# Cross attention's value products past the first superblock as split products of 512 tokens

## The chip, the core and the metric

The kernel runs on one core of one Trainium2 chip. The metric is the device time of one execution in microseconds (us). The core has a matrix engine (TensorE, PE in the profile, with its weight loads as PEld), a vector engine (VectorE, DVE), a scalar engine (ScalarE, ACT), GpSimd (POOL) and SyncE (SP), which here issues most of the DMA. TensorE reads on-chip memory (SBUF) and writes PSUM, which the others read.

## What is computed

One layer on 2048 tokens of width 1024: a norm, one wide input projection, three branches beside each other, and a gated merge that is projected once more and added to the input. The branches are an RWKV-7 recurrence (8 heads of 64), windowed attention with sinks (8 heads of 64), and cross attention into a memory of 256 tokens (4 heads of 128). The change is in the last one:

```python
def memory_cross_attn(q, mem, mem_norm_g, w_mem_kv, xq_g, xk_g):
    q = rms_norm(q.reshape(bsz, t, X_HEADS, X_HEAD_DIM), xq_g)
    kv = rms_norm(mem, mem_norm_g) @ w_mem_kv
    km, vm = kv[..., :X_WIDTH], kv[..., X_WIDTH:]
    km = rms_norm(km.reshape(bsz, m, X_HEADS, X_HEAD_DIM), xk_g)
    vm = vm.reshape(bsz, m, X_HEADS, X_HEAD_DIM)
    s = jnp.einsum('bthd,bmhd->bhtm', q, km).astype(jnp.float32) * (X_HEAD_DIM ** -0.5)
    p = jax.nn.softmax(s, axis=-1)
    o = jnp.einsum('bhtm,bmhd->bthd', p.astype(vm.dtype), vm)
    return o.reshape(bsz, t, X_WIDTH)
```

All is float32. The last `einsum`, probabilities times the memory's values, is called the value product below.

## The kernel before

**Tiles and split products.** The tokens are worked in four superblocks of 512 (`sb` 0 to 3). Most matrix products are split products: each operand is held as a rounded half of type f32r (ScalarE copies it with `AF.Copy`, which rounds) and the rest (DVE subtracts the rounded half from the original), and `gemm3` (L453 to L459) makes three products of the halves, high by high, high by rest, rest by high, into one PSUM bank. A few products are plain f32: transposes, the recurrence, and cross attention's value products (L1003).

**Weights.** In the first superblock a weight block is loaded raw, split, used, and stored split to DRAM (L438 to L443); later superblocks load the split block (L435). SP issues these loads and stores, in order, from one queue; there are 8 buffers (`whl`).

**Memory keys and values.** `mem_kv` runs once at the start. Keys are kept split in DRAM (`Kd`, named `mk`), values plain (`Vd`, named `mv`, L642): two tiles of 128 memory tokens by 512 channels.

**Two streams.** Within a superblock, `stream_r` (the recurrence: preparation, a forward substitution on DVE at L803 to L805 called the inverse below, then a chain of small products) and `stream_f` (four cross heads, then windowed attention woven with the merges, then gates) are written interleaved; the numbers that they yield and `PACE` set where one stands against the other. Then `order` plans the whole program: `lay_out` takes the next ready instruction of each engine by its rank, with costs of its own for each operation and the free buffers of each pool, and the resulting order of each engine is fixed. So an added or removed instruction can move others anywhere behind it. All engines work through their order without overtaking.

**A cross head** (`cross_head`, L948 on). Loads of the keys `km` and the values `vm` (two buffers of 128x2x128 each, 128 KB); the query projection; its split (L954, L955); statistics; scores by `gemm3`; maximum, exponential and denominators. Then the part in question: per half of 256 tokens, `scaled_by` scales two probability tiles (DVE, L934; in the first superblock ScalarE, L936), four transposes each of 128x128 (L999) put them into a PSUM bank `as_` (two such banks), ScalarE copies the bank to SBUF (L1001), and two plain f32 products of 256 tokens (L1003) accumulate over the 256 memory tokens into the bank `oo` (one such bank). Behind it, `silu2` (L923 to L929) makes the gate: projection into `mm` (two banks), a tanh on ScalarE (L927), a multiply on DVE (L928); L1006 multiplies it with the value product and `split_y` splits the result (L941, L942). The other intermediate tiles, `g2` in the code and `g` in the profile, share 11 buffers of 2 KB per partition.

## Time and profile before

| what | value |
|---|---|
| median of 3 runs | 2250.22 us (2249.85 to 2250.74) |
| profiled execution, own time | 2250.33 us |
| its span, first to last instruction | 2248.5 us |
| busy: PE, DVE, ACT, POOL | 99%, 68%, 41%, 7% of the span |
| mean granted TensorE clock | 0.997 of full |
| moved by DMA | 430.55 MB, mean 191 GB/s |

A timeline row gives start, duration, engine, line, operation, output<-inputs, shape and count, then in brackets the engine's idle time before it and what ended it. Durations of TensorE overlap, since its products are pipelined: what one costs is the difference to the start of the next. A wait row reads "who <- for whom: us in total, times, longest". A windows row gives the stretch, its length, then busy time and count of PE, PEld, DVE, ACT and POOL, the granted clock, the DMA share and GB/s. A chain row gives start, duration and what.

### The profile page before, as it was taken

How to read it: one execution, taken by the hardware profiler on the slowest of the kernel's cores; microseconds unless marked ns; L12 is line 12 of the kernel's file. 1: busy time of each engine (PE TensorE's matmuls, PEld its weight loads, DVE VectorE, ACT ScalarE, POOL GpSimd, SP SyncE). 2: the span in 40 equal slices, each digit the busy share in tenths (PEclk: the TensorE clock that was granted, in tenths of full speed). 3: DMA queues.
4: the chain of work that ended last, by engine and by line, in shares of the span. 5: the costliest groups of instructions: out<-in, count | busy, mean ns of one | idle time of the engine just before them, and what ended most of it. 6: DMA issues, size and time to landing. Idle time of an engine off the chain costs nothing.

```text
span 2248.5 us, 36875 instructions
## 1 busy us (share of the span) xinstructions
PE 2219.2 (99%) x13706; PEld 1806.1 (80%) x13706; DVE 1533.0 (68%) x3951; ACT 926.2 (41%) x2024; POOL 147.9 (7%) x209
## 2 busy tenths in 40 slices
PE   8999999999999999999999999999999999999999
PEld 7888778778888778878888878787888887787887
DVE  7799789775469777953437957985245895896312
ACT  6664565455253354423214345442223435434210
POOL 1000110000000011000000001000000001100000
PEclk9999999999999999999999999999999999999999
DMA  7777546679844444446774434445676444343655
GB/s 230 265 234 241 195 164 226 231 264 356 323 146 161 134 141 149 147 166 234 241 239 136 164 122 150 148 136 194 229 252 198 157 141 160 117 146 132 206 192 192
DMA packets 146226, 430.55 MB, mean 191 GB/s; under 512 B 16640, under 2 KB 21120, under 8 KB 146048
## 3 DMA queue, kind: packets, MB, share of 16 engines
q1 hardware_dynamic: 129920, 398.83, 52.6%
q10 hardware_dynamic: 16128, 29.37, 4.0%
q8 instruction: 109, 1.79, 0.3%
q14 instruction: 69, 0.57, 0.1%
HBM read 333.24 MB, written 94.90 MB: 190 GB/s over the span
## 4 chain that ended last, share of the span: by engine, by line
PE 74%; DVE 18%; ACT 3%; DMA 2%; issue 2%; POOL 1%; SPq 0%; DVEq 0%; ACTq 0%; POOLq 0%
PE mm L457 18%; PE mm L459 18%; PE mm L458 18%; DVE ibc L803 1%; PE rw L881 1%; DVE ibc L804 1%; ACT g L1102 1%; DVE Yi L805 1%; PE mm L1172 1%; PE mm L1174 1%; PE mm L1173 1%; PE oo L1003 1%; PE rw L866 1%; PE rw L874 1%; DVE g L1114 1%
## 5 line engine op out<-in xcount | busy, mean ns | idle before, releaser
L457 PE MATMUL mm<-hH,whl 128*128 128x512 f32 x1888 | 750.4, 397 | 5.8 <-DVE g L928 3.5
L459 PE MATMUL mm<-hH,whl 128*128 128x512 f32 x1888 | 748.9, 397 | 0.0
L458 PE MATMUL mm<-hL,whl 128*128 128x512 f32 x1888 | 748.7, 397 | 0.0
L457 PEld LDWEIGHTS mm<-hH,whl 128*128 128x128 f32 x1888 | 355.1, 188 | 77.9 <-DVE g L928 3.9
L459 PEld LDWEIGHTS mm<-hH,whl 128*128 128x128 f32 x1888 | 355.3, 188 | 69.4
L458 PEld LDWEIGHTS mm<-hL,whl 128*128 128x128 f32 x1888 | 355.3, 188 | 68.3 <-issue 0.7
L439 ACT ACTIVATE whl<-raw 128x512 fp32r<-128x512 f32 x178 | 111.2, 629 | 146.9 <-PE mm L459 80.1
L440 DVE TENSOR_TENSOR whl<-raw,whl 128x512 fp32r<-128x512 f32 x178 | 124.5, 702 | 50.6 <-ACT whl L439 49.5
L457 PE MATMUL mm<-yh,whl 128*128 128x512 f32 x384 | 151.3, 394 | 0.0
L458 PE MATMUL mm<-yl,whl 128*128 128x512 f32 x384 | 150.8, 393 | 0.0
L459 PE MATMUL mm<-yh,whl 128*128 128x512 f32 x384 | 150.7, 393 | 0.0
L872 ACT ACTIVATE SP<-Z,Pl 64x64 f32<-64x64 f32 x256 | 88.3, 345 | 115.0 <-DVE Z L882 111.4
L803 DVE STREAM_SHUFFLE ibc<-Nc 128x496 f32<-128x496 f32 (+30 forms) x248 | 113.4, 473 | 0.1
L1155 DVE SCALAR_TENSOR_TENSOR g<-g,mm 128x512 f32<-128x512 f32 x32 | 21.8, 681 | 128.6 <-PE mm L459 128.5
L804 DVE TENSOR_TENSOR ibc<-ibc,Yi 128x496 f32<-128x496 f32 (+30 forms) x248 | 104.5, 421 | 3.9
L805 DVE TENSOR_TENSOR Yi<-Yi,ibc 128x496 f32<-128x496 f32 (+30 forms) x248 | 103.2, 416 | 0.9
L882 DVE SCALAR_TENSOR_TENSOR Z<-rw,Pl,SP 64x64 f32<-64x64 f32 x224 | 63.5, 284 | 51.1 <-PE rw L881 47.5
L1140 ACT ACTIVATE gt<-mm 128x512 f32<-128x512 f32 x64 | 38.0, 593 | 144.1 <-PE mm L459 143.8
L457 PEld LDWEIGHTS mm<-yh,whl 128*128 128x128 f32 x384 | 72.1, 188 | 15.0 <-DVE g L1155 0.4
L459 PEld LDWEIGHTS mm<-yh,whl 128*128 128x128 f32 x384 | 72.1, 188 | 14.6
L458 PEld LDWEIGHTS mm<-yl,whl 128*128 128x128 f32 x384 | 72.1, 188 | 14.3
L1102 ACT ACTIVATE g<-g,mxs,st 128x256 f32<-128x256 f32 (+1 forms) x128 | 74.5, 584 | 18.4 <-DVE mxs L1095 18.2
(1902 smaller groups left out, 3783.9 us busy)
## 6 DMA issues: line engine op xcount, KB each, us to landing
whl<-k SPq DMA_DIRECT2D x486, 512.0 KB, 3.3
k<-whl SPq DMA_DIRECT2D x162, 512.0 KB, 4.4
raw<-in_w_in SPq DMA_DIRECT2D x118, 256.0 KB, 3.3
g<-in_x ACTq DMA_DIRECT2D x32, 256.0 KB, 4.4
out<-g ACTq DMA_DIRECT2D x32, 256.0 KB, 4.5
raw<-in_w_proj SPq DMA_DIRECT2D x24, 256.0 KB, 3.1
rt<-in_x ACTq DMA_DIRECT2D x24, 256.0 KB, 5.7
rt<-in_xt ACTq DMA_DIRECT2D x24, 256.0 KB, 5.8
```

Of the source, the lines that this page charges most:

```text
L439: S.activation(w[:, 0], raw, AF.Copy)
L440: V.tensor_tensor(w[:, 1], raw, w[:, 0].bitcast(F32), op=ALU.subtract)
L457: PE.matmul(out, lh, rh, start=i == 0, stop=False)
L458: PE.matmul(out, lh, rl, start=False, stop=False)
L459: PE.matmul(out, ll, rh, start=False, stop=i == n - 1)
L803: V.stream_shuffle(bc[:, :, :w], N_[:, :, s + 1:], [s] * 32)
L804: V.tensor_tensor(bc[:, :, :w], bc[:, :, :w], Y[:, :, s:s + 1].to_broadcast([128, n, w]), op=ALU.mult)
L805: V.tensor_tensor(Y[:, :, s + 1:], Y[:, :, s + 1:], bc[:, :, :w], op=ALU.add)
L872: S.activation(SP[h, i], Z[h, i, e, c], AF.Copy, scale=g[4][h, c:c + 1])
L882: upds = [V.scalar_tensor_tensor(Sst[h, g[0]] if c == NC_ - 1 else Z[h, i, e, c + 1], pS[h, i, e], g[4][h, c:c + 1], SP[h, i], op0=ALU.mul ...
L1102: S.activation(prs[b][:, i, m0:], prs[b][:, i, m0:], AF.Exp, scale=r2[:, b, i:i + 1], bias=mx[:, b, i:i + 1], accum_out=mx[:, b, 2 + i:3 + i])
L1140: S.activation(t, gp, AF.Tanh, scale=0.5)
```

## The change

Past the first superblock a head scales all four probability tiles first, makes for each half of the memory tokens (`kt`) four transposes into one bank of 512 tokens, splits that bank (ScalarE copies the rounded half, DVE subtracts), and makes one split product of 512 tokens per `kt`: six f32r products in place of four plain f32 ones of 256 tokens. The values are therefore also kept split in DRAM (`Vs`, named `mvs`), which `mem_kv` writes in four stores. The value tile grows to 128x2x2x128 (256 KB) and has one buffer in place of two. The first superblock computes as before, from the plain values, in a half of the larger tile.

```diff
+    Vs = dp.tile([128, 2, 2, 512], F32, name="mvs")
...
             nc.sync.dma_start(Vd[:, i], t)
+            p = [g2(F32R), g2(F32R)]
+            S.activation(p[0], o[i], AF.Copy)
+            V.tensor_tensor(p[1], o[i], p[0].bitcast(F32), op=ALU.subtract)
+            for u in range(2):
+                nc.sync.dma_start(Vs[:, u, i], p[u].bitcast(F32))
...
-        vm = rp.tile([128, 2, 128], F32, name="vm", bufs=2)
-        nc.sync.dma_start(vm, Vd[:, :, h * 128:(h + 1) * 128])
+        if sb:
+            vm = rp.tile([128, 2, 2, 128], F32R, name="vm", bufs=1)
+            nc.sync.dma_start(vm.bitcast(F32), Vs[:, :, :, h * 128:(h + 1) * 128])
+        else:
+            vm = rp.tile([128, 2, 2, 128], F32, name="vm", bufs=1)[:, 0]
+            nc.sync.dma_start(vm, Vd[:, :, h * 128:(h + 1) * 128])
...
+        if not sb:
...
+        else:
+            for q in range(4):
+                scaled_by(prs[q // 2][:, q % 2], dn[:, q:q + 1], sb)
+            pts = []
+            for kt in range(2):
+                pt = s_ps()
+                for q in range(4):
+                    PE.transpose(pt[:, q * 128:(q + 1) * 128], prs[q // 2][:, q % 2, kt * 128:(kt + 1) * 128], ident)
+                pts.append((g2(F32R), g2(F32R)))
+                S.activation(pts[kt][0], pt, AF.Copy)
+                V.tensor_tensor(pts[kt][1], pt, pts[kt][0].bitcast(F32), op=ALU.subtract)
+            oo = o_ps()
+            gemm3(oo, [((vm[:, 0, kt], vm[:, 1, kt]), pts[kt]) for kt in range(2)])
```

What the planner makes of it is shown at three places. In the changed kernel L1022 is the transpose, L1025 the subtraction, L1030 the old L1006, L934 the old L928, L940 the old L934, L809 to L811 the old L803 to L805, L727 the old L721; the split value products are those of L457 to L459 with output `oo`.

TensorE at head 0 of the second superblock, from its last transposes on, before:

```order
L999 MATMUL as__6868<-c_ident,g_6793 128x128 x2
L999 MATMUL as__6879<-c_ident,g_6796 128x128 x4
L458 MATMUL mm<-hL,whl 128x512
L459 MATMUL mm<-hH,whl 128x512
L457 MATMUL mm<-hH,whl 128x512
L458 MATMUL mm<-hL,whl 128x512
L1003 MATMUL oo<-g_6875,vm 128x256 x2
L1003 MATMUL oo<-g_6886,vm 128x256 x2
```

and now (`g_6889` is a rounded half, `g_6890` its rest):

```order
L1022 MATMUL as__6884<-c_ident,g_6809 128x128
L1022 MATMUL as__6893<-c_ident,g_6809 128x128
L458 MATMUL mm<-hL,whl 128x512
L459 MATMUL mm<-hH,whl 128x512
L457 MATMUL mm<-hH,whl 128x512
L458 MATMUL mm<-hL,whl 128x512
L459 MATMUL mm<-hH,whl 128x512
L457 MATMUL mm<-hH,whl 128x512
L457 MATMUL oo<-g_6889,vm 128x512
L458 MATMUL mm<-hL,whl 128x512
L459 MATMUL mm<-hH,whl 128x512
L458 MATMUL oo<-g_6890,vm 128x512
```

The value products moved two dense products back, and the second one, the first that needs the rest, two more.

DVE at head 2 of the second superblock, from its last scalings on, before (in the middle of the inverse):

```order
L934 TENSOR_SCALAR g_7364<-g_7364,dn 128x256 x2
L804 TENSOR_TENSOR ibc<-ibc,Yi 128x16x27
L803 STREAM_SHUFFLE ibc<-Nc 128x16x26
L805 TENSOR_TENSOR Yi<-Yi,ibc 128x16x27
L804 TENSOR_TENSOR ibc<-ibc,Yi 128x16x26
L803 STREAM_SHUFFLE ibc<-Nc 128x16x25
```

and now:

```order
L940 TENSOR_SCALAR g_7389<-g_7389,dn 128x256 x2
L811 TENSOR_TENSOR Yi<-Yi,ibc 128x16x27
L809 STREAM_SHUFFLE ibc<-Nc 128x16x26
L809 STREAM_SHUFFLE ibc<-Nc 128x16x25
L810 TENSOR_TENSOR ibc<-ibc,Yi 128x16x26
L1025 TENSOR_TENSOR g_7449<-as__7443,g_7448 128x512
L1025 TENSOR_TENSOR g_7458<-as__7452,g_7457 128x512
```

TensorE at the same head, from its last transposes on, before:

```order
L999 MATMUL as__7426<-c_ident,g_7364 128x128 x4
L459 MATMUL mm<-hH,whl 128x512
L457 MATMUL mm<-hH,whl 128x512
L458 MATMUL mm<-hL,whl 128x512
L459 MATMUL mm<-hH,whl 128x512
L1003 MATMUL oo<-g_7422,vm 128x256 x2
```

and now:

```order
L1022 MATMUL as__7452<-c_ident,g_7389 128x128 x2
L457 MATMUL mm<-hH,whl 128x512
L458 MATMUL mm<-hL,whl 128x512
L459 MATMUL mm<-hH,whl 128x512
L457 MATMUL mm<-hH,whl 128x512
L458 MATMUL mm<-hL,whl 128x512
L457 MATMUL oo<-g_7448,vm 128x512
L459 MATMUL mm<-hH,whl 128x512
L457 MATMUL mm<-hH,whl 128x512
L458 MATMUL mm<-hL,whl 128x512
L459 MATMUL mm<-hH,whl 128x512
L458 MATMUL oo<-g_7449,vm 128x512
```

Two subtractions are new on DVE in the middle of the inverse, four of whose steps stand before them, and the second value product has five plus four dense products between it and the transposes.

DVE in the first superblock, in the preparation of the recurrence's second group of heads, with the gate of a windowed head (L928) in it. The last rows before L928, before:

```order
L728 SCALAR_TENSOR_TENSOR QO<-rt,Pt 64x8x64
L730 SCALAR_TENSOR_TENSOR rt<-rt 128x512
L735 TENSOR_TENSOR rk__2989<-rk__2989,rt 128x512
L440 TENSOR_TENSOR whl<-raw,whl 128x512
L732 TENSOR_TENSOR BK<-rt 64x8x64
L742 TENSOR_TENSOR QE<-rr__3114,Pt 64x8x64
L732 TENSOR_TENSOR BK<-rt 64x8x64
L440 TENSOR_TENSOR whl<-raw,whl 128x512
L928 SCALAR_TENSOR_TENSOR g_3505<-g_3505,mm 128x512
```

and now, from the first row (L727, the old L721) that reads the statistics from PSUM:

```order
L727 TENSOR_SCALAR dk<-rw 64x4
L734 SCALAR_TENSOR_TENSOR QO<-rt,Pt 64x8x64
L727 TENSOR_SCALAR dk<-rw 64x4
L736 SCALAR_TENSOR_TENSOR rt<-rt 128x512
L727 TENSOR_SCALAR dk<-rw 64x4
L748 TENSOR_TENSOR QE<-rr__3127,Pt 64x8x64
L728 RECIPROCAL dk<-dk 128x8
L738 TENSOR_TENSOR BK<-rt 64x8x64
L741 TENSOR_TENSOR rk__3002<-rk__3002,rt 128x512
L440 TENSOR_TENSOR whl<-raw,whl 128x512
L934 SCALAR_TENSOR_TENSOR g_3518<-g_3518,mm 128x512
```

Ahead of this piece stand one more L727 and one more L440. Before, the rows of `dk` stood far ahead of L928, with two more products of the recurrence's output (L916, L917) among them; now they stand right before it. On TensorE the products that make those statistics stood nine dense products ahead of the projection that L928 reads, and stand twelve into its 24 now.

More of the change, by code (lines that the diff above doesn't have):

```diff
@@ L991, in cross_head @@
         yield 5.667
[L992 to L1003 removed]
+        if not sb:
+            oo = o_ps()
+            for t2 in range(2):
+                pt = s_ps().rearrange("p (k i t) -> p k i t", k=2, i=2)
+                for i in range(2):
+                    q = 2 * t2 + i
+                    scaled_by(prs[t2][:, i], dn[:, q:q + 1], sb)
+                    for kt in range(2):
+                        PE.transpose(pt[:, kt, i], prs[t2][:, i, kt * 128:(kt + 1) * 128], ident)
+                pts = g2(shape=(128, 2, 256))
+                S.activation(pts.rearrange("p k t -> p (k t)"), pt.rearrange("p k i t -> p (k i t)"), AF.Copy)
+                for kt in range(2):
+                    PE.matmul(oo[:, t2 * 256:(t2 + 1) * 256], vm[:, kt], pts[:, kt], start=kt == 0, stop=kt == 1)
+        else:
+            for q in range(4):
+                scaled_by(prs[q // 2][:, q % 2], dn[:, q:q + 1], sb)
+            pts = []
+            for kt in range(2):
+                pt = s_ps()
[4 more added lines that the diff above has]
+                V.tensor_tensor(pts[kt][1], pt, pts[kt][0].bitcast(F32), op=ALU.subtract)
+            oo = o_ps()
+            gemm3(oo, [((vm[:, 0, kt], vm[:, 1, kt]), pts[kt]) for kt in range(2)])
         yield 3
```

10 lines of the change are left out of this document (removed).

## The prediction

> **What bounds the kernel now.** I read the page's busy times and slices first, then the chain of work that ended last.
>
> ```profile
> span 2248.5 us, 36875 instructions
> PE 2219.2 (99%) x13706; PEld 1806.1 (80%) x13706; DVE 1533.0 (68%) x3951; ACT 926.2 (41%) x2024; POOL 147.9 (7%) x209
> PE   8999999999999999999999999999999999999999
> DVE  7799789775469777953437957985245895896312
> PE 74%; DVE 18%; ACT 3%; DMA 2%; issue 2%; POOL 1%; SPq 0%; DVEq 0%; ACTq 0%; POOLq 0%
> ```
>
> TensorE has work in every slice. VectorE (DVE) is full in some slices and half idle in others, and holds 18% of the chain. So the time is the sum of what TensorE must stream, plus the places where it waits. All listed waits of TensorE come to about 26 us; the two largest groups are these:
>
> ```profile
> PE mm L457 <- DVE g L928: 3.5, 1, 3.5
> PE rw L770 <- DVE whl L761: 2.5, 4, 1.1
> ```
>
> None of the listed waits after the first superblock stands at cross attention's value products. A cheaper product there is therefore worth its own TensorE time, unless a new wait eats it.
>
> **What goes and what comes on TensorE.** The timeline of TensorE at head 2 of the second superblock, with the old products (L1003) between two stretches of dense products:
>
> ```profile
> 707.33 1.89 PE L1003 MATMUL oo<-g,vm 128*128 128x256 f32 x8
> 708.87 0.58 PE L457 MATMUL mm<-hH,whl 128*128 128x512 f32 x1
> 709.28 0.39 PE L458 MATMUL mm<-hL,whl 128*128 128x512 f32 x1
> ...
> 711.59 0.39 PE L459 MATMUL mm<-hH,whl 128*128 128x512 f32 x1
> ```
>
> Durations overlap, so I take differences of starts. From 709.28 to 711.59 there are ten dense products, 0.23 us each. From 707.33 to 709.28 are 1.95 us, in which one dense product (L457) and the eight L1003 records lie: the eight cost 1.95 - 0.23 = 1.72 us, 0.215 each. Each plain f32 product of 256 tokens appears as two records. In its place come six split products of 512 tokens, the form of those dense ones: 6 x 0.23 = 1.38 us. Saved: 0.34 us a head. The group row gives the number of heads:
>
> ```profile
> L1003 PE MATMUL oo<-g,vm 128*128 128x256 f32 x128 | 30.8, 379 | 0.6 <-ACT g L1001 0.6
> ```
>
> 128 records are 16 heads of 8; the first superblock keeps its 4. **12 x 0.34 = 4.1 us saved.** The transposes stay eight a head and of one size (128x128), so I count them at no difference. What the switch between the two kinds of product costs is inside the 1.95 us.
>
> [...]
>
> **What comes on the other engines.** ScalarE's two copies of 512 columns a head stay two. DVE gets two subtractions of 128x512 from PSUM a head; the kernel makes the same operation for the queries (L955):
>
> ```profile
> 647.98 0.69 DVE L955 TENSOR_TENSOR g<-mm,g 128x512 fp32r<-128x512 f32 x1
> ```
>
> 24 x 0.69 = 16.6 us more on DVE, 1.4 a head. What hides them differs by head. At head 0 DVE has nothing to do there:
>
> ```profile
> 642.47 0.68 DVE L778 TENSOR_TENSOR rt<-rr__6859,rt 128x512 fp32r<-128x512 f32 x1
> 645.75 0.69 DVE L1006 TENSOR_TENSOR gt<-oo,gt 128x512 f32<-128x512 f32 x1 [2.60 <-PE oo L1003]
> L1001 ACT ACTIVATE g<-as__6868 x1: 599/599/599, 642.6 to 642.6; 128x512 f32<-128x512 f32 x1
> 642.82 0.48 PE L458 MATMUL mm<-hL,whl 128*128 128x512 f32 x1
> ```
>
> The rounded half is ready at 642.6 + 0.6 = 643.2 and the rest at 643.9, inside the idle 2.60 us. The new order puts six dense products, the first value product and two more dense ones behind the transposes, which end at about 642.8: the product that needs the rest starts at 642.8 + 9 x 0.23 = 644.9, a us after it is there. No wait. At heads 2 and 3 DVE is full:
>
> ```profile
> 680.00:730.00 50.00, 50.00 (x272) 41.75 (x270) 48.75 (x134) 18.45 (x43) 2.71 (x5) 1.00 0.48 161
> 706.09 0.66 DVE L803 STREAM_SHUFFLE ibc<-Nc 128x416 f32<-128x416 f32 x1
> 706.64 0.58 DVE L805 TENSOR_TENSOR Yi<-Yi,ibc 128x432 f32<-128x432 f32 x1
> 705.96 0.60 PE L999 MATMUL as__7426<-c_ident,g 128*128 128x128 f32 x4
> 706.32 0.47 PE L459 MATMUL mm<-hH,whl 128*128 128x512 f32 x1
> ```
>
> (In the first row the columns behind the span are the busy times of PE, PEld, DVE, ACT and POOL; DVE has 48.75 of 50.) At head 2 the new order of DVE puts four steps of the inverse, 0.55 us from start to start, between the last scaling and the two subtractions: the first rest is there 4 x 0.55 + 0.69 = 2.9 us after the scaling. On TensorE four transposes (706.32 - 705.96 = 0.36 us), nine dense products and the first value product stand between that scaling and the second value product, which needs the rest: 0.36 + 10 x 0.23 = 2.7 us. That is even, and a small wait follows. Nothing shows it before; its bounds are 0 and the whole subtraction pair, 1.4 us. I take 0.1 us at heads 2 and 3, nearest to the row of head 0: **+0.6 us** in all. What queues behind the subtractions is the inverse (L803 to L805), so the recurrence starts 1.4 to 2.8 us later in each superblock; TensorE has other streams' dense products to fill with, as it has 50.00 of 50 us in that row.
>
> **The loads.** One buffer of 256 KB in place of two of 128 KB: a head's load may now be issued only when the value products of the head before are done, so its time must fit between two heads.
>
> ```profile
> 643.99 1.73 PE oo L1003 x8
> 667.55 1.73 PE oo L1003 x8
> 707.49 1.73 PE oo L1003 x8
> 727.73 1.73 PE oo L1003 x8
> vm<-mv SPq DMA_DIRECT2D x16, 128.0 KB, 2.5
> SPq L951 <- PE oo L1003: 43.9, 12, 4.8
> ```
>
> The shortest distance is 20.2 us, the load lands in 2.5 us, and twice the bytes in at most 5. The last row says that SP's queue already stood at 12 of these loads, 3.7 us each, for value products of an earlier head, with the weight loads queued behind, and TensorE lists no wait for it. I count 0; the bound is one such stand of 4.8 us at a place where weights run short.
>
> **The memory's part.** Two copies on ScalarE, two subtractions and four stores of 256 KB at about 50 us.
>
> ```profile
> mv<-g SPq DMA_DIRECT2D x2, 256.0 KB, 5.0
> 0.00:60.00 60.00, 54.22 (x287) 46.73 (x288) 42.39 (x113) 37.33 (x81) 11.15 (x27) 0.91 0.72 240
> ```
>
> The last two numbers are the DMA share and GB/s. 1 MB at 240 GB/s is 4.4 us of transfer, with 28% of the share free; a bound of 4.4 us therefore, and 0 below. TensorE keeps working there on weights loaded before, so I take **+0.3 us**, near the lower end.
>
> **The sum.** The profiled execution took 2250.33 us by its own time, span 2248.5; the median of three runs is 2250.22, the same within 0.1. 2250.3 - 4.1 + 0.6 + 0.3 = **2247.1 us**. A measurement of this kernel tells about 0.2% (4.5 us) from no change, so this saving, if it comes as worked out, lies within it.
>
> **Rivals.** (a) *A stall in the first superblock goes, or only its clock loss.* One TensorE wait there is dear:
>
> ```profile
> 289.23 0.15 DVE L721 TENSOR_SCALAR dk<-rw 64x4 f32<-64x4 f32 x1
> 299.02 0.69 DVE L928 SCALAR_TENSOR_TENSOR g<-g,mm 128x512 f32<-128x512 f32 x1
> 295.87 0.39 PE L459 MATMUL mm<-hH,whl 128*128 128x512 f32 x1
> 299.76 0.53 PE L457 MATMUL mm<-hH,whl 128*128 128x512 f32 x1 [3.50 <-DVE g L928]
> 300.10 0.62 PE L458 MATMUL mm<-hL,whl 128*128 128x512 f32 x1
> 300.51 0.63 PE L459 MATMUL mm<-hH,whl 128*128 128x512 f32 x1
> 300.00:304.00 4.00, 4.00 (x15) 2.77 (x16) 3.42 (x8) 1.50 (x5) 0.00 (x0) 0.57 0.65 211
> ```
>
> 3.5 us idle, and then products at 0.41 instead of 0.23 us at a granted clock of 0.57 over 4 us, another 1.7 us. [...] All 5.2 us are freed if DVE's L928 comes early enough: 2247.1 - 5.2 = **2241.9**; the clock loss alone, 2245.4. The new order changes this place. TensorE makes the statistics on which the first dk row (L721) waits 21 dense products later, 12 before the end of the projection that L928 reads. From that dk row to the twin of L928 stand seven operations of 0.69 us and five small ones of 0.15 (itself among them), 5.6 us, where before it was 299.02 - 289.23 = 9.8. So the twin begins 5.6 - 12 x 0.23 = 2.8 us behind the projection's end; before it began 299.02 - 296.1 = 2.9 behind. The stall stays, most likely. Chance 0.12.
>
> (b) *DVE becomes the bound in the later superblocks.* The chain of the second superblock runs through DVE for over 100 us, here its first and last piece,
>
> ```profile
> 818.39 0.73 DVE g L573 x2
> 926.81 0.61 DVE g L509
> ```
>
> and DVE may reach it 1.4 us late per subtraction pair. If nothing hides any pair, all 16.6 us show: 2247.1 + 16.6 - 0.6 = 2263.1; if half does, **2254.8**, slower than before. It decides from 4.1 / 3 = 1.4 us of new wait per superblock on. For it: DVE 48.75 of 50. Against it: the window of 800 to 900 us leaves DVE a fifth idle,
>
> ```profile
> 800.00:900.00 100.00, 98.40 (x588) 80.01 (x587) 79.80 (x184) 45.22 (x100) 12.40 (x16) 1.00 0.44 148
> ```
>
> and TensorE idles only 1.6 us there. Chance 0.14.
>
> (c) *The saving is given back.* The products are cheaper, but TensorE waits for the rest halves by the same 0.34 us, or the rearranged first superblock loses as much: **2250.3**. Chance 0.16.
>
> (d) *The new products stream faster than the dense ones,* at the 0.215 us that the eight old records show: 12 x (1.72 - 1.29) = 5.2 saved, **2246.0**; chance 0.06. [...]
>
> **How the numbers follow.** The forecast has 0.52, with its own range 2245 to 2249, of which I put 0.12 below 2245.7 (a saving of over 0.2%). Faster by over 0.2%: 0.12 from (a), 0.12 of the forecast, 0.03 of (d): 0.27. Slower by over 0.2%, above 2254.7: 0.09 of (b), 0.02 of (c): 0.11. Within: 0.62. The range runs from 2242.5 (leaving out half of (a)) to 2253 (leaving out most of (b)): it takes in +4.4 of the memory's part and, with the other sums, the bound of 4.8 us.
>
> **What would show it.** Right: a head's six products between dense ones cost 1.38 us from start to start, no wait of over 0.3 us at the second of them, waits of TensorE at about 26 us in all, the 3.5 us wait in the first superblock still there, with the reduced clock behind it. Wrong: six products far from 1.38 us; new waits for DVE that recur in three superblocks at the same place; the clock row lower or higher than before; waits for weights behind the load of the values.

## The result, and the profile after

The changed kernel took 2252.99 us (median of 22 executions, 2249.59 to 2259.96), the kernel before beside it 2250.83 (22 executions, 2249.66 to 2253.55). The ratio is 1.0014, 95% interval 1.0008 to 1.0020: a little slower, though within the 0.2% that I had set as the bound. 2247.1 was forecast. The spread is part of the result: it was 3.9 us before and is 10.4 us now. The profiled execution of the changed kernel took 2254.41 us by its own time, 4.1 more than the profiled one of before, where the medians differ by 2.2: nine of the 22 executions had a mean granted clock of 0.996 or less, with a median of 2256.07, and the profiled one is among them; the other 13 have a median of 2251.84.

The page of the changed kernel, its busy times and the engines' shares of the chain of work that ended last:

```profile
span 2252.3 us, 36907 instructions
PE 2216.2 (98%) x13682; PEld 1803.8 (80%) x13682; DVE 1548.9 (69%) x3977; ACT 922.0 (41%) x2024; POOL 154.7 (7%) x209
PE 75%; DVE 18%; ACT 2%; DMA 2%; issue 1%; POOL 1%; SPq 0%; DVEq 0%; ACTq 0%; POOLq 0%
```

TensorE has less to do (24 matmuls fewer, 3.0 us less busy) and the span is 3.8 us longer. Both can only hold if it waits more. The waits of TensorE in the changed kernel, those that are new or longer:

```profile
PE mm L457 <- DVE g L934: 4.6, 1, 4.6
PE rw L759 <- DVE QO L748: 2.9, 3, 1.0
PE rw L791 <- DVE carry L667: 2.5, 3, 0.8
PE as__3855 L1110 <- DVE g L1084: 1.6, 1, 1.6
PE as__19826 L511 <- DVE g L509: 0.9, 1, 0.9
PE as__9438 L511 <- DVE g L509: 0.9, 1, 0.9
PE as__14632 L511 <- DVE g L509: 0.9, 1, 0.9
```

Three of them come once in each later superblock (L759, L791, L511: 1.0, 0.8 and 0.9 us); two stand in the first superblock (L457 with 4.6 us in place of 3.5, and L1110 with 1.6, which is new). None stands at the value products, and none is for a weight or a value tile. All listed waits of TensorE add up to about 31 us, against about 25 before.

To see how much each stretch gained or lost I cut all traces at the same places. A superblock ends where its output projection starts its last product (L1174 before, L1198 in the changed kernel); its output phase begins at its last transposes of the recurrence's result (L525), and in the last superblock, which has none there, three dense products before the first product of `yh` (2178.40 us before, 2182.36 in the changed kernel). Windows from the end of one superblock to the next output phase, the three later superblocks summed, before:

```profile
sum 1437.36, PE 1429.22 PEld 1160.05 DVE 976.98 ACT 567.19 POOL 99.63; mean PE 476.41 PEld 386.68 DVE 325.66 ACT 189.06 POOL 33.21
```

and in the changed kernel:

```profile
sum 1436.79, PE 1424.94 PEld 1155.22 DVE 991.31 ACT 564.75 POOL 105.48; mean PE 474.98 PEld 385.07 DVE 330.44 ACT 188.25 POOL 35.16
```

The first number is the length, the next the busy time of TensorE, so the difference is its idle time. TensorE saves 4.3 us there, as the forecast's 4.1 said, and idles 11.85 in place of 8.14 us, 3.7 more. So 0.6 us is left of the saving. The other 4.5 us of difference stand in the first superblock: it ends at 608.1 us before and at 612.6 in the changed kernel. TensorE's idle time there is 19.6 in place of 16.6 us, and the clock is halved (granted 0.50) for 17.1 in place of 13.7 us. In such a stretch a dense product starts every 0.43 us (300.16 to 304.43 us in the changed kernel, ten steps) in place of 0.23. Half clock for 3.4 us more therefore costs 1.7 us, an estimate of half its length, and 3.0 + 1.7 = 4.7 us is about what is seen. This is a balance of two things: in the first 25 us of the program the clock is halved for 3.4 us in place of 10.2, and at 300 and 340 us for 13.7 in place of 3.4, so a better start hides part of what these two places cost. The output phases differ by 0.3 us in all.

These are the two places in the changed kernel's timeline where the first superblock's new waits stand, with what is beside them. The first three rows show the wait for the windowed head's gate (L934, the old L928), the last two the new wait at L1110:

```profile
299.57 0.80 PE L457 MATMUL mm<-hH,whl 128*128 128x512 f32 x1 [4.62 <-DVE g L934]
300.16 0.63 PE L458 MATMUL mm<-hL,whl 128*128 128x512 f32 x1
300.58 0.63 PE L459 MATMUL mm<-hH,whl 128*128 128x512 f32 x1
...
337.40 0.95 PE L499 MATMUL as__3843<-c_bones,g 128*128 128x2 f32 x8
339.99 0.45 PE L1110 MATMUL as__3855<-KsH,g 128*128 128x128 f32 x1 [1.64 <-DVE g L1084]
```

and the two windows of halved clock:

```profile
298.70:305.53 6.83, 5.96 (x16) 4.39 (x18) 5.96 (x14) 1.12 (x2) 0.00 (x0) 0.50 0.32 115
339.65:346.48 6.83, 6.50 (x43) 6.08 (x44) 5.07 (x14) 0.24 (x1) 1.91 (x2) 0.50 0.90 299
```

The seventh value, 0.50, is the granted clock. Before, there was one such window of 3.41 us at 300 us and none at 340.

### The profile page after: what moved, and what is told of

It is laid out like the page before. It is cut to its first block, busy times and chain, and to the rows that moved or that the text cites. A ratio compares the mean times of both kernels' runs of the same rounds, so it can differ in the third digit from the quotient of the medians.

```text
span 2252.3 us, 36907 instructions
## 1 busy us (share of the span) xinstructions
PE 2216.2 (98%) x13682; PEld 1803.8 (80%) x13682; DVE 1548.9 (69%) x3977; ACT 922.0 (41%) x2024; POOL 154.7 (7%) x209
## 4 chain that ended last, share of the span: by engine, by line
PE 75%; DVE 18%; ACT 2%; DMA 2%; issue 1%; POOL 1%; SPq 0%; DVEq 0%; ACTq 0%; POOLq 0%
PE mm L459 18%; PE mm L458 18%; PE mm L457 18%; DVE ibc L809 2%; PE rw L887 1%; PE mm L1196 1%; PE mm L1198 1%; PE mm L1197 1%; PE rw L872 1%; DVE Yi L811 1%; PE oo L1152 1%; DVE ibc L810 1%; PE rw L880 1%; DVE whl L440 1%; POOL st L426 1%
## 5 line engine op out<-in xcount | busy, mean ns | idle before, releaser
L457 PE MATMUL mm<-hH,whl 128*128 128x512 f32 x1888 | 750.5, 398 | 5.9 <-DVE g L934 4.6
L459 PE MATMUL mm<-hH,whl 128*128 128x512 f32 x1888 | 749.1, 397 | 0.0
L457 PEld LDWEIGHTS mm<-hH,whl 128*128 128x128 f32 x1888 | 355.5, 188 | 77.3 <-DVE g L934 5.0
L459 PEld LDWEIGHTS mm<-hH,whl 128*128 128x128 f32 x1888 | 355.5, 188 | 69.4
L440 DVE TENSOR_TENSOR whl<-raw,whl 128x512 fp32r<-128x512 f32 x178 | 122.8, 692 | 46.8 <-ACT whl L439 45.2
L457 PE MATMUL mm<-yh,whl 128*128 128x512 f32 x384 | 151.4, 394 | 0.4 <-DVE g L1179 0.4
L459 PE MATMUL mm<-yh,whl 128*128 128x512 f32 x384 | 151.1, 393 | 0.0
L809 DVE STREAM_SHUFFLE ibc<-Nc 128x496 f32<-128x496 f32 (+30 forms) x248 | 113.1, 472 | 0.0
L811 DVE TENSOR_TENSOR Yi<-Yi,ibc 128x496 f32<-128x496 f32 (+30 forms) x248 | 103.3, 417 | 1.0
L457 PEld LDWEIGHTS mm<-yh,whl 128*128 128x128 f32 x384 | 72.2, 188 | 15.1 <-DVE g L1179 1.0
L459 PEld LDWEIGHTS mm<-yh,whl 128*128 128x128 f32 x384 | 72.1, 188 | 14.8
```

The lines of the kernel that those rows point to most:

```text
L440: V.tensor_tensor(w[:, 1], raw, w[:, 0].bitcast(F32), op=ALU.subtract)
L457: PE.matmul(out, lh, rh, start=i == 0, stop=False)
L459: PE.matmul(out, ll, rh, start=False, stop=i == n - 1)
L809: V.stream_shuffle(bc[:, :, :w], N_[:, :, s + 1:], [s] * 32)
L811: V.tensor_tensor(Y[:, :, s + 1:], Y[:, :, s + 1:], bc[:, :, :w], op=ALU.add)
```

## The experiments

Theory A: the value products save what was worked out; the later superblocks lose it because the subtractions of heads 2 and 3 stand inside the inverse, where VectorE is full (busy for 48.75 of the 50 us from 680 to 730 us before, for 48.59 of those from 684 to 734 us in the changed kernel), and the first superblock loses because the memory's part and the single larger value buffer make the planner lay it out differently. Rival B: the memory's part costs the time. Rival C: any new order of the program shifts waits about, and nothing in particular is to blame. The table has all runs, cut as above: the profiled execution's first superblock (its end, TensorE's idle time in it, the halved clock up to its end), the three later ones up to their output phases (length, TensorE busy, idle), then the median of all executions and the ratio to the kernel before with its 95% interval.

| kernel | end | idle | half clock | length | busy | idle | us | ratio |
|---|---|---|---|---|---|---|---|---|
| before | 608.1 | 16.6 | 13.7 | 1437.4 | 1429.2 | 8.1 | 2250.8 | |
| changed | 612.6 | 19.6 | 17.1 | 1436.8 | 1424.9 | 11.9 | 2253.0 | 1.0014 (1.0008 to 1.0020) |
| memory's part alone | 606.1 | 17.0 | 10.2 | 1437.0 | 1429.1 | 7.9 | 2248.7 | 0.9991 (0.9983 to 1.0000) |
| no memory's part | 606.2 | 16.3 | 6.8 | 1436.8 | 1425.0 | 11.8 | 2249.0 | 0.9992 (0.9984 to 1.0001) |
| no subtractions | 610.0 | 20.2 | 10.2 | 1433.6 | 1426.5 | 7.1 | 2249.1 | 0.9999 (0.9990 to 1.0008) |
| heads 0 and 1 only | 611.2 | 21.1 | 13.7 | 1436.0 | 1427.3 | 8.7 | 2252.2 | 1.0008 (0.9999 to 1.0017) |
| two value tiles | 607.7 | 17.0 | 6.8 | 1437.4 | 1425.5 | 11.9 | 2248.9 | 0.9993 (0.9985 to 1.0002) |
| scalings on ScalarE | 612.9 | 19.2 | 20.5 | 1432.5 | 1424.9 | 7.6 | 2248.2 | 0.9994 (0.9985 to 1.0003) |
| two tiles, scalings on ScalarE | 606.1 | 16.8 | 6.8 | 1432.3 | 1424.7 | 7.5 | 2243.7 | 0.9975 (0.9966 to 0.9984) |
| gate copied by ScalarE | 611.7 | 19.3 | 17.1 | 1436.8 | 1425.0 | 11.8 | 2252.6 | 1.0010 (1.0001 to 1.0018) |
| memory's part and larger buffer | 608.8 | 19.3 | 10.2 | 1437.4 | 1429.0 | 8.4 | 2254.7 | 1.0020 (1.0011 to 1.0029) |
| the same again | 615.9 | 20.6 | 23.9 | 1437.1 | 1428.8 | 8.3 | 2256.4 | 1.0017 (1.0007 to 1.0027) |
| before, scalings on ScalarE | 606.8 | 17.1 | 6.8 | 1435.9 | 1429.1 | 6.8 | 2250.3 | 0.9997 (0.9988 to 1.0006) |
| all three mends | 606.7 | 17.9 | 3.4 | 1432.4 | 1424.8 | 7.6 | 2242.0 | 0.9960 (0.9947 to 0.9972) |

### The memory's part alone

The kernel before, with `Vs`, its two copies, subtractions and four stores, and nothing that reads it.

> The kernel before, with only the memory's part added: two copies, two subtractions and four stores of the split values, which nothing reads. Theory A (the loss has two places: the first superblock in its new order with a longer wait and more half clock, and new waits of TensorE for DVE in the later superblocks): TensorE's order in the first superblock stays almost that of before, so the time is that of before within 0.6 us, and the end of the first superblock's output stays at 607 to 608 us. Rival B (the memory's part itself, its transfers and copies, costs the first superblock its 4.5 us): 3 to 4.5 us over before.

2248.74 us: no cost. The first superblock ends 2 us earlier than before. By the same estimate 1.7 us of this are the clock, halved for 10.2 us in place of 13.7: for 3.4 in place of 10.2 at the start, for 6.8 in place of 3.4 near 295 us. TensorE's order in the first superblock is the same in both traces but for a few rows, and the halved clock also differs between two profiles of one program below (10.2 and 23.9 us), so this gain isn't put down to the edit. Rival B is out.

### No memory's part

```diff
-            nc.sync.dma_start(vm.bitcast(F32), Vs[:, :, :, h * 128:(h + 1) * 128])
+            for u in range(2):
+                nc.sync.dma_start(vm[:, u].bitcast(F32), Vd[:, :, h * 128:(h + 1) * 128])
```

`Vs` and all that writes it go as well.

> The changed kernel without the memory's part; the later superblocks load the plain values into both halves, so their result is not the reference's, with the same number of products and bytes. TensorE's order in the first superblock is almost that of before. Theory A: the first superblock ends at about 608 us instead of 612, the later ones last 545.85, 545.5 and 544.1 as in the changed kernel: 0.9 us below before. Rival C (re-planning alone moves waits at random, in any superblock): no such agreement, 2 us around before on either side.

2249.02 us. The first superblock is back at 606.2, with its idle time at 16.3. The later ones are the changed kernel's, with all of the 3.7 us of added idle time. So the single larger buffer alone does not disturb the first superblock, nor does the memory's part alone.

### No subtractions

```diff
-                pts.append((g2(F32R), g2(F32R)))
-                S.activation(pts[kt][0], pt, AF.Copy)
-                V.tensor_tensor(pts[kt][1], pt, pts[kt][0].bitcast(F32), op=ALU.subtract)
+                ph = g2(F32R)
+                S.activation(ph, pt, AF.Copy)
+                pts.append((ph, ph))
```

> The changed kernel without the 24 subtractions of probabilities on DVE: the rounded half stands in for the rest, six products a head as before; the result is not the reference's. The first superblock is in the same order as in the changed kernel. Theory A: first superblock 612 us as in the changed kernel, and the later superblocks get the whole saving of 1.4 us each (544.3, 544.5, 543.3), the inverse's first burst of small products at 148 us of a superblock instead of 151.7, and no wait of 0.9 us at L511: 3 us below the changed kernel, about 2250. Rival C: the waits in the later superblocks stay at about 1 us each, the time that of the changed kernel.

The later superblocks fall by 3.2 us against the changed kernel and are 3.8 below before. The first one stays late at 610.0. The waits in this kernel:

```profile
PE mm L457 <- DVE g L934: 4.6, 1, 4.6
PE as__3855 L1110 <- DVE g L1084: 1.6, 1, 1.6
PE rw L791 <- DVE dns L1129: 1.1, 3, 0.4
```

Both waits of the first superblock are still there. L791 waits 0.4 in place of 0.8 us a superblock, the wait of L759 for `QO`, 1.0 us in each later superblock, is gone. A wait of 0.9 us at L511 is still there, against what theory A expected, but at another product some 50 us earlier in the superblock. The two losses have two causes.

### Split products at heads 0 and 1 only

```diff
-        if sb:
+        if sb and h < 2:
...
-        if not sb:
+        if not sb or h > 1:
```

and the old path for the others.

> The split value products only at heads 0 and 1 of the later superblocks, where DVE has idle time beside them; heads 2 and 3, beside the inverse, as before. Theory A: half the saving (0.7 us a superblock) without the later inverse: superblocks of about 545.1, 545.2 and 544.0, first burst at 148 us, first superblock 612 us as in the changed kernel: 1 us below the changed kernel. Rival C: waits as in the changed kernel, so half a saving less, 2 us above the changed kernel.

TensorE saves 1.9 us, half of 4.3 but for 0.25, and idles 0.5 more: 1.4 us net from these two heads. The changed kernel has 0.6 net from four. Heads 2 and 3 therefore save 2.4 us and pay 3.2, a loss of 0.8. Those are the two that stand inside the inverse. In the whole time the step is not clear: the interval of the ratio overlaps the changed kernel's.

### Two value tiles in place of one

```diff
-            vm = rp.tile([128, 2, 2, 128], F32R, name="vm", bufs=1)
-            nc.sync.dma_start(vm.bitcast(F32), Vs[:, :, :, h * 128:(h + 1) * 128])
+            vm = [rp.tile([128, 2, 128], F32R, name="vm", bufs=2) for _ in range(2)]
+            for u in range(2):
+                nc.sync.dma_start(vm[u].bitcast(F32), Vs[:, u, :, h * 128:(h + 1) * 128])
...
-            vm = rp.tile([128, 2, 2, 128], F32, name="vm", bufs=1)[:, 0]
+            vm = rp.tile([128, 2, 128], F32, name="vm", bufs=2)
...
-            gemm3(oo, [((vm[:, 0, kt], vm[:, 1, kt]), pts[kt]) for kt in range(2)])
+            gemm3(oo, [((vm[0][:, kt], vm[1][:, kt]), pts[kt]) for kt in range(2)])
```

The same space as two buffers of 128 KB, so that the first superblock has its two buffers again and TensorE's order there is that of the kernel with the memory's part alone.

> Past the first superblock the values are held as two tiles of 128 KB (rounded half and rest, two loads) in the two old buffers, so that the first superblock has two buffers of 128 KB again and its planned order on TensorE is that of the kernel with the memory's part alone. All else is as in the changed kernel. Theory A (the change lost about 4 us in the first superblock because the single larger buffer, together with the memory's new work, re-planned it; the later superblocks gain only about 1 us in all because the subtractions stand inside the inverse): first superblock's output phase at about 606 us as with the memory's part alone (before 608.1, changed kernel 612.6), later superblocks as in the changed kernel, 545.9, 545.5 and 544.1 us; time about 2248.5 to 2249.5, 1 to 2 us below before. Rival C (any new order of the program loses a few us somewhere, the buffer has nothing to do with it): the first superblock ends at 610 us or later, time 2252 or above. Rival D (the single buffer costs in the later superblocks too, since a head's load waits for the head before): the later superblocks shorten by more than 0.5 us each against the changed kernel.

As theory A had it, but for a first superblock that ends at 607.7 in place of 606: 2248.93 us, the idle time of the first superblock 17.0. The place near 300 us reads as before, 3.5 us and one window of 3.41:

```profile
298.04 0.50 PE L457 MATMUL mm<-hH,whl 128*128 128x512 f32 x1 [3.49 <-DVE g L934]
```

The later superblocks are unchanged, so rival D falls: one buffer or two is the same to them.

### The scalings on ScalarE

```diff
-                scaled_by(prs[q // 2][:, q % 2], dn[:, q:q + 1], sb)
+                scaled_by(prs[q // 2][:, q % 2], dn[:, q:q + 1], 0)
```

> As the changed kernel, but the four scalings a head past the first superblock are on ScalarE in place of VectorE; the subtractions stay. Theory A (VectorE's load inside the inverse is what eats the saving of the later superblocks, whatever the operation): heads 2 and 3 put 8 scalings of 256 columns fewer on VectorE, about as much time as their 4 subtractions add, so the inverse's first products come back from 151.7 to about 148 us behind the superblock's start and the later superblocks fall to about 544.4, 544.7 and 543.8 us, as without the subtractions; the first superblock stays at about 612 us; time about 2249 to 2250. Rival E (it is the wait of the second value product for its rest half, a latency, and not VectorE's load): the later superblocks stay at 545.9, 545.5 and 544.1 us, or grow since ScalarE's queue delays the transposes; time about 2253.

The subtractions stay, and the idle time of the later superblocks falls from 11.9 to 7.6 us nevertheless. So it was VectorE's load inside the inverse that cost, not the latency of a rest half; rival E falls. Whole, they took 543.7, 543.8 and 542.8 us, 2.6 us less in all than theory A had said from the kernel without subtractions. Their idle time is not lower than there (7.6 against 7.1): 1.3 us of the difference are in the output phases and 1.6 in TensorE's busy time (1424.9 against 1426.5), and why that one is higher without subtractions is not shown. The median, 2248.16, is also about 1 us lower than expected, with the first superblock still at 612.9.

### Two value tiles and the scalings on ScalarE

Both edits above.

> The values as two tiles of 128 KB in the two old buffers and the four scalings a head past the first superblock on ScalarE; all else as in the changed kernel. Theory A: both losses go. First superblock at about 606 us, later ones about 544.4, 544.7 and 543.8 us, time about 2245 to 2246, some 4 to 5 us below before (ratio 0.998). Rival C (a new order loses a few us somewhere): 2249 or above. Rival E (the loss of the later superblocks is a latency at the second value product): later superblocks 545.9, 545.5 and 544.1 us, time about 2249.

2243.74 us, below the kernel before by 0.25% (0.16 to 0.34) and somewhat below the 2245 to 2246 that theory A had. Its later superblocks in one row:

```profile
sum 1432.27, PE 1424.74 PEld 1155.02 DVE 979.01 ACT 587.21 POOL 102.85; mean PE 474.92 PEld 385.01 DVE 326.34 ACT 195.74 POOL 34.28
```

VectorE has 979.0 us, 2 more than before the change, in place of 14.3 more; ScalarE has 20 more and is at 41% of the stretch. The forecast's saving is there in full, 5.1 us with the relief.

### The kernel before with the scalings on ScalarE

Nothing of the change; only the last argument of `scaled_by` becomes 0. It tells what the split products are worth beside the relief.

> The kernel before, with nothing of the change, but the four scalings a head past the first superblock on ScalarE in place of VectorE. It tells how much of the gain of the fastest kernel so far (two value tiles and scalings on ScalarE, 2243.7 us) is the split products' and how much any relief of VectorE gives. Theory A (VectorE bounds only the stretch of the inverse; once it is relieved the split products are worth their 4.2 us): first superblock as before at 606 to 608 us, the inverse's first products at about 145 us instead of 148, later superblocks 2 to 3 us shorter in all, time 2247 to 2248.5; the split products then account for the other 4. Rival F (the relief of VectorE is the whole gain, and the split products give nothing even then): later superblocks 5 to 6 us shorter in all, time 2243.5 to 2245.5. Rival E (no gain from ScalarE by itself): 2250 to 2251.

The later superblocks fall by 1.5 us, less than the 2 to 3 expected, and the median (2250.34) shows nothing: its interval reaches from -0.1% to +0.1%. Against it, the last kernel is 1435.85 - 1432.27 = 3.6 us shorter in that stretch. So with VectorE relieved the split products are worth 3.6 of the 4.3 us that they save on TensorE, and rival F falls. The inverse's first products are at 145.0 us of the superblock, as expected. The whole times set the two kernels further apart (ratios 0.9975 and 0.9997, about 5 us), and this profile is of the fastest of its 11 executions (2247.07 us), so what is beyond the 3.6 us is open.

### The gate copied by ScalarE

```diff
+        if copy:
+            c = g2()
+            S.activation(c, o, AF.Copy)
+            o = c
...
-        z = silu2(B_ZB + j, hT)
+        z = silu2(B_ZB + j, hT, copy=not sb)
```

> As the changed kernel, but in the first superblock ScalarE copies a windowed head's gate projection out of PSUM and VectorE's multiply reads the copy, so that TensorE's next projection no longer waits for VectorE to free the bank; the result is the same, with 8 copies of 512 columns more on ScalarE. Theory A (the first superblock of the changed kernel loses by a wait of 4.6 us for that multiply and by the halved clock that goes with it): no wait of over 2 us there, at most 3.4 us of halved clock at 295 to 305 us, the first superblock's output phase at 606 to 609 us instead of 612.6, time 2247 to 2250. Rival C (the wait only moves, to VectorE's next late product, since VectorE is what is late): the first superblock stays at 610 to 613 us with another wait of 2 to 5 us close by, time 2251 to 2254.

Mostly a miss for theory A's sharper form. The waits of this kernel near 300 us and behind, then ScalarE's tanh (L933) and copy (L936) of that gate:

```profile
299.68 0.50 PE L457 MATMUL mm<-hH,whl 128*128 128x512 f32 x1 [2.77 <-ACT g L936]
312.05 0.51 PE L457 MATMUL mm<-hH,whl 128*128 128x512 f32 x1 [1.41 <-DVE carry L667]
297.97 0.60 ACT L933 ACTIVATE g<-mm 128x512 f32<-128x512 f32 x1
299.05 0.58 ACT L936 ACTIVATE g<-mm 128x512 f32<-128x512 f32 x1
```

The wait fell from 4.6 to 2.8 us and is now one for ScalarE: the projection ends at 296.9, the tanh runs from 297.97 to 298.57, and the copy starts at 299.05. At 312 us another wait, for VectorE, grew from 0.2 to 1.4 us. The idle time of the first superblock is 19.3, as good as unchanged, and the median 2252.58. The time is where rival C had it, but the wait moved to ScalarE first and only in part to VectorE's next late product; the copy also changes TensorE's order, so which of the two keeps the idle time is not shown.

### The memory's part and the larger buffer, with the old products

```diff
-        vm = rp.tile([128, 2, 128], F32, name="vm", bufs=2)
+        vm = rp.tile([128, 2, 2, 128], F32, name="vm", bufs=1)[:, 0]
```

on top of the memory's part alone. TensorE's order through the first superblock is then the changed kernel's, row by row, and no product is split.

> The kernel before with two parts of the change only: the memory's values are also stored split (and never read), and the value tile is one buffer of 256 KB, of which the plain values fill half. The products are the old plain ones everywhere. The planned order of TensorE in the first superblock is then the changed kernel's, row by row. Theory A (it is this order of the first superblock that loses 4 to 5 us, and no split product is needed for it): the first superblock's output phase at 610 to 613 us, with a wait of about 4.7 us for the windowed head's gate near 300 us, the later superblocks at about 545.7, 546 and 544.6 us as before; time 2252 to 2255, slower than before. Rival C (the loss of the first superblock was chance of the runs, or came from the split products): first superblock at 606 to 608 us, time 2249 to 2251.

2254.71 us, slower by 0.20% (0.11 to 0.29). The time is where theory A put it, but this profile has 3.1 us of it in the output phases (67.2 to 67.5 us each in the later superblocks, 66.1 to 67.1 in the profiles of before and of the memory's part alone), and its first superblock ends at 608.8 in place of 610 or later. So I took a second profile.

> The kernel with the memory's part and the single larger buffer alone, a second time, for a second profile. In the first one the output phases at the end of the later superblocks took 67.2 to 67.5 us against 66.0 to 67.1 in the other kernels, and the first superblock lost less than its order was expected to. If that was chance of one execution: output phases of the later superblocks at 65.8 to 66.7 us this time, and the first superblock's output phase at 608 to 613 us. If the single buffer does it: 67 us or more again in all three.

The output phases were 66.3, 67.2 and 65.7 this time. Two of three are back, and the kernel with two value tiles and the scalings on ScalarE, which has no single buffer, has one of 67.2 too: chance of the execution, most likely. The first superblock ended at 615.9, seven us later than in the first profile of the same program, with nearly the same waits. First profile:

```profile
298.96 0.79 PE L457 MATMUL mm<-hH,whl 128*128 128x512 f32 x1 [4.51 <-DVE g L934]
338.91 0.30 PE L1092 MATMUL as__3855<-KsH,g 128*128 128x128 f32 x1 [1.67 <-DVE g L1066]
```

second profile:

```profile
302.37 0.79 PE L457 MATMUL mm<-hH,whl 128*128 128x512 f32 x1 [4.55 <-DVE g L934]
342.79 0.44 PE L1092 MATMUL as__3855<-KsH,g 128*128 128x128 f32 x1 [1.67 <-DVE g L1066]
```

and the second profile's windows:

```profile
260.44:263.85 3.41, 3.41 (x10) 2.90 (x11) 2.07 (x9) 2.93 (x10) 0.00 (x0) 0.50 0.72 231
301.40:308.23 6.83, 5.86 (x16) 4.25 (x18) 6.07 (x14) 1.02 (x2) 0.00 (x0) 0.50 0.34 115
342.36:349.19 6.83, 6.41 (x43) 5.99 (x44) 5.16 (x14) 0.33 (x1) 1.91 (x2) 0.50 0.83 305
```

In the first profile only the middle one of these was halved. Halved clock before the end of the first superblock is 10.2 us in one and 23.9 in the other; half of the difference is 6.8 us, and the ends differ by 7.0. This is the loss of the first superblock: in the six profiles with its new order TensorE waits more (19.2 to 21.1 us of idle time in the table, in place of 16.3 to 17.1 in the six with the other order, the copies of the gate left out), and the clock is often halved for longer. In all executions with that order (changed, no subtractions, heads 0 and 1, scalings on ScalarE, and these two), 31 of 75 had a mean granted clock of 0.996 or less; of the kernels with the other order (memory's part alone, no memory's part, the two with two tiles, before with ScalarE), 0 of 55, and of the kernel before itself, run beside these experiments, 4 of 98.

### All three mends

Two tiles, scalings on ScalarE, and the copy of the gate.

> Two value tiles, scalings past the first superblock on ScalarE, and in the first superblock the copy of the windowed heads' gate projections by ScalarE, so that the next projection doesn't wait for VectorE's multiply. Theory A: the wait of 3.5 us near 298 us falls to 2 us or less and half a window of reduced clock goes with it; first superblock at 603 to 605 us, later ones as with the two tiles and ScalarE, time 2241 to 2243. Rival C (the wait moves to VectorE's next late product, as the run with the copy alone showed, where it fell from 4.6 to 2.8 us and others rose): 2243 to 2245, no gain over the kernel without the copy.

2241.99 us (5 executions), the lowest of the study, 0.40% below before (0.28 to 0.53). The copy's own share is open: the interval overlaps that of the kernel without it, and the first superblock of its profile ends no earlier (606.7 against 606.1), with no halved clock near 300 us (1.00 from 290 to 310 us) but 1.1 us more idle time.

## Why the prediction was wrong, point by point

**The saving on TensorE: right.** 4.1 us was forecast, and 4.3 us of busy time went. Head 2 of the second superblock, in the changed kernel:

```profile
713.45 0.39 PE L459 MATMUL mm<-hH,whl 128*128 128x512 f32 x1
713.68 0.39 PE L458 MATMUL oo<-g,vm 128*128 128x512 f32 x1
713.91 0.39 PE L459 MATMUL oo<-g,vm 128*128 128x512 f32 x1
714.13 0.39 PE L457 MATMUL oo<-g,vm 128*128 128x512 f32 x1
714.36 0.39 PE L458 MATMUL oo<-g,vm 128*128 128x512 f32 x1
714.59 0.39 PE L459 MATMUL oo<-g,vm 128*128 128x512 f32 x1
714.81 0.39 PE L457 MATMUL mm<-hH,whl 128*128 128x512 f32 x1
```

From 713.68 to 714.81 are five value products, 0.226 us each: six are 1.36 us (1.38 forecast). Rival (d), 0.215, is out.

**The wait at the second value product: none.** I had put 0.6 us there. The subtraction that it needs:

```profile
L1025 DVE TENSOR_TENSOR g<-as__7443,g x1: 672/672/672, 712.7 to 712.7; 128x512 fp32r<-128x512 f32 x1
```

The rest is there at 713.4 and the product starts at 713.68, with no idle time before it. The size of a subtraction was right as well (0.67 against 0.69).

**What queues behind the subtractions: this step failed.** The prediction said that the inverse would end 1.4 to 2.8 us later and that TensorE "has other streams' dense products to fill with", and counted nothing. The first products on the finished inverse, before and in the changed kernel:

```profile
755.74 0.69 PE L819 MATMUL rw<-ibc,AB 32*32 32x32 f32 x32
```

```profile
763.88 0.69 PE L825 MATMUL rw<-ibc,AB 32*32 32x32 f32 x32
```

From the superblock's start that is 755.74 - 608.12 = 147.6 and 763.88 - 612.62 = 151.3 us, 3.6 us later. TensorE did fill that hole: it was busy for all of the 16.48 us from 747.40 to 763.88. But the recurrence's second group then met a VectorE that was late, and the price was paid at L759, L791 and L511, 75 to 146 us behind that place: 2.7 us a superblock in place of about 1.5 us of waits that stood in that stretch before, with other small shifts 3.7 us more in all. The four kernels with all subtractions and scalings on VectorE (changed, no memory's part, two value tiles, gate copied) have the inverse's first products at 151.2 to 151.3 us and 11.8 to 11.9 us of idle time; the five that take the subtractions, the scalings or the new work of heads 2 and 3 off it have 147.4 to 147.9 us and 7.1 to 8.7. That the late inverse itself makes the waits at L759 and L791 is argued from this; the wait at L511 stays in one kernel whose inverse is in time, so its cause is open. That is rival (b)'s mechanism at a quarter of its whole price, and it is the sign of being wrong that the prediction named: new waits for DVE at the same place of three superblocks. The prediction's point from which it decides was 1.4 us a superblock; 1.2 came. I had set it aside by VectorE's fifth of idle time between 800 and 900 us, an average over a stretch in which single waits decide.

**The first superblock: this step failed too.** I judged one place of it (L934 for L928), from the planned order, and found "the stall stays". It grew by 1.1 us. The eight small products that the statistics come from, the projection's last product, and then VectorE's rows, in the changed kernel:

```profile
291.17 0.95 PE L499 MATMUL rw<-c_bones,rt 128*128 128x2 f32 x8
294.56 0.39 PE L459 MATMUL mm<-hH,whl 128*128 128x512 f32 x1
```

```profile
292.05 0.68 DVE L734 SCALAR_TENSOR_TENSOR QE<-rt,Pt 64x512 f32<-64x512 f32 x1
292.65 0.15 DVE L727 TENSOR_SCALAR dk<-rw 64x4 f32<-64x4 f32 x1
...
297.27 1.52 DVE L440 TENSOR_TENSOR whl<-raw,whl 128x512 fp32r<-128x512 f32 x1
298.82 0.69 DVE L934 SCALAR_TENSOR_TENSOR g<-g,mm 128x512 f32<-128x512 f32 x1
```

I had 5.6 us of VectorE from the first `dk` row on, less 2.8 of TensorE. It took 298.82 - 292.65 = 6.2 us, since one subtraction took 1.52 us where I had 0.69 (why isn't shown; before, L730 had taken 1.44 in that stretch, and I had 0.69 for all), and it began 0.5 us after the statistics were there (291.17 + 0.95 = 292.1), since L734 stood before it. So L934 began 3.9 us behind the projection's end at 294.95. Worse, I read no other place of a superblock in which some 230 of TensorE's first 2600 rows had moved: the new wait of 1.6 us at L1110 and the halved clock that stands beside both waits were not in the sum. This part is the larger of the two: 4.5 us in the profiled execution, though with a clock below that of most executions.

**The loads and the memory's part: right as transfers.** TensorE waits for no value tile, and the memory's part alone costs nothing (0.3 forecast). But I counted the buffer at 0, and it is what changes the plan: together with the memory's part it costs 4.2 us without any split product. As a piece of SBUF it was free; as an input to the planner it was not.

**Rivals and the range.** (c), "the saving is given back", with 2250.3 and a chance of 0.16, comes nearest, 2.7 us too low: by the second way that it names, the rearranged first superblock, and not by the first, since nothing waits for the rest halves. The later superblocks lost by (b)'s mechanism instead. (a) had the sign wrong: the stall grew from 3.50 to 4.62 us and the halved clock beside it from 3.41 to 6.83. That a wait and the halved clock behind it go together was my reading of one trace: beside the wait of 1.67 us in the two profiles of one program there are 6.83 us of it in one and none in the other. The forecast was a gain and the kernel is slower, beyond the interval. That 2252.99 lies in the range that ended at 2253 is luck: its upper part stood for the memory's transfers and a late load, neither of which cost anything. The listed waits before add up to about 25 us, not the 26 that the prediction has, which changes nothing in its sum.

## What to carry to other kernels

Work added to an engine that is full in one stretch was paid here where that engine's results were next needed (2.7 us a superblock), not where the work stands: follow the delay to the end of the chain, as the waits 75 to 146 us later show, and before adding work to such a stretch move other work off it (here the scalings: with two value tiles, moving them turned -0.07% into -0.25%). Where a planner fixes the order, a buffer count is an edit to the whole program: compare the order in stages that the change doesn't touch, and price all the moved rows or none. A wait on TensorE is to be priced with the clock: the same 1.67 us stood beside a full clock in one execution and beside 6.83 us of half clock, worth an estimated 3.4 us, in another.

## What the runs showed of the hardware

The granted clock was 0.50 in these stretches of the first superblock:

| profile | start, us | length, us |
|---|---|---|
| before | 13.37 | 10.24 |
| before | 300.09 | 3.41 |
| changed | 18.80 | 3.41 |
| changed | 298.69 | 6.83 |
| changed | 339.65 | 6.83 |
| memory's part and larger buffer, second profile | 260.44 | 3.41 |
| the same | 301.40 | 6.83 |
| the same | 342.36 | 6.83 |

The last profile has 6.8 us more of it elsewhere in the first superblock (23.9 - 17.1).

What stood beside them differs. In the kernel before, the stretch at 300.09 us began 0.3 us after a wait of 3.50 us had ended (299.76). In the changed kernel the one at 298.69 us began within the wait of 4.62 us that ended at 299.57; the one at 339.65 us began within the wait of 1.64 us that ended at 339.99, and ahead of that wait stood 0.95 us of products of two columns (L499, from 337.40 on). In the two profiles of one program the same products of two columns (0.95 us) and the same wait of 1.67 us follow each other: in the second profile the wait ended at 342.79 and the clock was halved for 6.83 us from 342.36 on, in the first it ended at 338.91 and the clock was 1.00 from 338 to 348 us. What decides between the two was not shown.
